# Output projection: sums of weight quadrants made by accumulating transfers from GpSimd's queue instead of by VectorE

## The chip, the cores and the metric

The kernel runs on one core of one Trainium2 chip. The metric is the time of one execution on the device in microseconds (us). A core has TensorE (PE), VectorE (DVE), ScalarE (ACT), GpSimd (POOL) and SyncE (SP), each with an instruction queue of its own that is worked off in order, and 16 DMA engines that carry the transfers which those queues issue. Engines wait for each other by semaphores.

## What is computed

A decoder layer over 512 tokens of width 2048 in float32: windowed attention and a gated DeltaNet branch, side by side, are merged and go through an output projection.

```python
y_a = a_out @ w_o_swa
y_b = o.reshape(B, T, DN_VAL).astype(x.dtype) @ w_o_dn
y = jax.nn.sigmoid(mg_a) * y_a + jax.nn.sigmoid(mg_b) * y_b
return x + gate * (y @ w_out)
```

The change touches only the last product, `y @ w_out`, with `y` of 512 x 2048 and `w_out` of 2048 x 2048.

## The kernel before

Every large product is made in three matmul passes: `split` (L52 and L53) cuts a float32 tile into a rounded high part, which ScalarE writes (`whi`), and a low part, which VectorE writes as source minus high part (`wlo`). `mm3` (L240 to L242) then multiplies high by high, high by low and low by high into the same PSUM tile.

`finish` makes the merged `y` column tile by column tile, and then calls `output`. There the last product is made by a scheme with seven quadrant products in place of eight. The four quadrants of `w_out` are halves of its rows by halves of its columns; `load` brings three of them at a time as two 1 MB tiles each: slot "a" (tile `raw`, from a pool of two buffers that the earlier stages used too), slot "b" (`rawb`) and slot "c" (`rawc`). The work runs over two halves `n` of each quadrant's columns. In each half the seven products come in the order m1, m7, m5, m2, m6, m4, m3 (the list `order`), and each product has four pieces `p` of 128 x 1024 weights. `piece(slot, p)` is such a piece. One piece feeds 12 matmuls.

The weights of m7, m6 and m4 are sums of quadrants. They are made in place, piece by piece: for m7, a becomes a + b, and b then becomes b + c; for m6, a becomes a + c; for m4, b becomes b + a. m5 uses the a that m7's first sum left. Slot b is loaded anew after m7 (for m2), and a, b and c are loaded for the second half after m4 and m3 (`after`). VectorE makes the sums, in `prep`, just before the piece is split.

`prep(i + 2)` is called after the first half of item `i`, so weights are prepared two pieces ahead of PE; `whi` and `wlo` have three buffers. Beside this run `combos` (L1309 to L1319), a generator that is advanced once an item and makes the sums of `y`'s quadrants on VectorE (tiles `ya`, `yc`, split into `hh`, `hl`), and `evict` and `columns` (L1397 to L1433), which take finished products out of PSUM on VectorE and ScalarE, scale them by the gate, add the residual `x` on GpSimd (L1400) and store the result by SP.

The instructions of each engine are placed by a scheduler from the order in which the program is written and from the dependences between tiles; semaphore waits follow from those. All transfers of the kernel before are issued by SP.

Of the kernel before, what the change touches and what calls it, by code (L numbers as in the profile page):

```python
# [11 lines left out]
ALU = mybir.AluOpType  # L12
# [24 lines left out]
class Layer:  # L37
# [1288 lines left out]
    def output(self, es, wk, A):  # L1326

        tc, nc, a = self.tc, self.nc, self.a
# [4 lines left out]
        def load(slot, c, r, nchunk):  # L1333

            for i in range(2):
                if slot == "a":
                    t = self.wraw.tile([P, 2048], F32, tag="raw", name="raw")
                else:
                    t = fr.tile([P, 2048], F32, tag=f"{slot}{i}", name=f"raw{slot}")
                nc.sync.dma_start(out=t, in_=a["w_out"][2 * c + nchunk, 2 * r + i])  # L1340
                slots[slot, i] = t

        piece = lambda slot, p: slots[slot, p // 2][:, (p % 2) * 1024 : (p % 2) * 1024 + 1024]

        def add(x, y):
            def f(p):
                nc.vector.tensor_tensor(out=piece(x, p), in0=piece(x, p), in1=piece(y, p), op=ALU.add)

            return f

        order = [
            ("m1", "a11", "a", []),
            ("m7", "s3", "b", [add("a", "b"), add("b", "c")]),
            ("m5", "s1", "a", []),
            ("m2", "a12", "b", []),
            ("m6", "s2", "a", [add("a", "c")]),
            ("m4", "a22", "b", [add("b", "a")]),
            ("m3", "s4", "c", []),
        ]
        items = [(n, m, p) for n in range(2) for m in range(7) for p in range(4)]  # L1360
# [6 lines left out]
        def prep(i):  # L1367
            if i >= len(items):
                return
            n, m, p = items[i]  # L1370
            name, _, slot, sums = order[m]
            for f in sums:
                f(p)
            hi = self.whl.tile([P, 1024], F32R, tag="whi", name="whi")
            lo = self.whl.tile([P, 1024], F32R, tag="wlo", name="wlo")
            self.split(hi, lo, piece(slot, p))
            ready[i] = (hi, lo)
            for s, c, r in after.get((name, p), []):
                if name == "m7":
                    load(s, c, r, n)  # L1380
                elif n == 0:
                    load(s, c, r, 1)
# [53 lines left out]
        for i in range(2):  # L1436
            prep(i)
        for i, (n, m, p) in enumerate(items):
            name, s, slot, _ = order[m]
            if p == 0:  # L1440
                for t in range(2):
                    m7 = name == "m7"
                    ps[name, t] = pf.tile([P, T], F32, tag=f"y{t}" if m7 else "r", name=name, bufs=1 if m7 else 6)
            hi, lo = ready.pop(i)
            ah, al = A[s]
            for kk in range(2):
                kt = 2 * p + kk
                w = slice(kk * T, kk * T + T)
                for t in range(2):
                    tsl = slice(t * P, (t + 1) * P)  # L1450
                    self.mm3(ps[name, t], (ah[:, kt, tsl], al[:, kt, tsl]), (hi[:, w], lo[:, w]), kt == 0, kt == 7)
                if kk == 0:
                    prep(i + 2)
                    for f in todo:
                        evict(*f)
                    todo = []
                    next(side, None)
            if p == 3:
                todo.append((n, name))
# [108 lines left out]
```

## Time and profile before

| | |
|---|---|
| time, median of 3 runs | 2930.38 us (2930.1 to 2932.3) |
| span of the profiled execution | 2929.7 us, mean granted PE clock 0.995 |
| median less that span | 0.7 us |
| busy: PE, VectorE, ScalarE, GpSimd | 2870.6, 1787.2, 1085.1, 243.0 us |
| moved by DMA | 451.11 MB, mean 154 GB/s |
| first and last matmul of the output projection start at | 2752.3 and 2921.4 us |

The page gives the profiled execution by its span, from the first to the last instruction; the runs are timed without a profile. Rows of a timeline give start, duration, engine, source line, operation, output and inputs, and in brackets the idle time before and what ended it. The rows of windows give, for each engine, the busy time and the number of instructions in a stretch, then PE's granted clock, the mean busy share of the 16 DMA engines and what they moved.

### The profile page before, as it was taken

Reading aid. Unit: us, or ns where it says so; the run is one execution under the profiler, and the core shown is the slowest. Engines: PE = TensorE matmul, PEld = TensorE weight load, DVE = VectorE, ACT = ScalarE, POOL = GpSimd, SP = SyncE. Lnnn points to the kernel's source line nnn. Section 1 sums busy time; section 2 is a strip of 40 time slices with the busy share of each in tenths; the row PEclk is TensorE's granted clock in tenths of the full one; section 3 lists DMA queues with packets and bytes.
Section 4 is the critical chain, followed back from the end, with each engine's and each line's share of the span. In section 5 each row is a group of like instructions: output and inputs, shape, how many; then the busy total and the mean of one; then the engine's idle time right before and its main releaser. Section 6 shows DMA issues by size and latency. Waiting matters only on the chain.

```text
span 2929.7 us, 38073 instructions
## 1 busy us (share of the span) xinstructions
PE 2870.6 (98%) x14556; PEld 2351.2 (80%) x14556; DVE 1787.2 (61%) x2915; ACT 1085.1 (37%) x2113; POOL 243.0 (8%) x204
## 2 busy tenths in 40 slices
PE   8899999999999999999999999999999999999988
PEld 6677888888888888888888788888787877888867
DVE  6775998777776545544444553434655655553697
ACT  4355333333334333333333322212343443432343
POOL 0022211100000110000000000000100000000022
PEclk9999999999999999999999999999999999999999
DMA  9747555633334533333332675554322223375562
GB/s 387 281 147 219 163 169 159 203 109 111 125 113 134 160 116 124 115 122 109 123 109 100 235 263 182 186 172 141 105 89 94 85 89 103 119 262 172 173 194 97
DMA packets 175046, 451.11 MB, mean 154 GB/s; under 512 B 72433, under 2 KB 74993, under 8 KB 138897
## 3 DMA queue, kind: packets, MB, share of 16 engines
q1 hardware_dynamic: 174866, 448.70, 46.1%
q8 instruction: 114, 1.87, 0.3%
q14 instruction: 66, 0.54, 0.1%
HBM read 386.95 MB, written 59.45 MB: 152 GB/s over the span
## 4 chain that ended last, share of the span: by engine, by line
PE 84%; DVE 3%; DMA 2%; issue 1%; ACT 1%; POOL 1%; SPq 0%; POOLq 0%; DVEq 0%; ACTq 0%
PE mm L240 24%; PE mm L242 24%; PE mm L241 24%; DVE wlo L53 1%; PE S L1208 1%; PE pv L918 1%; PE po L937 1%; PE O L1259 1%; PE pP L274 1%; PE po L936 1%; PE pd L933 1%; PE pp L908 1%; PE m L241 1%; PE m L242 1%; PE m L240 1%
## 5 line engine op out<-in xcount | busy, mean ns | idle before, releaser
L240 PE MATMUL mm<-hh,whi 128*128 128x512 f32 x2784 | 1130.7, 406 | 2.3 <-ACT whi L52 1.6
L242 PE MATMUL mm<-hh,wlo 128*128 128x512 f32 x2784 | 1089.6, 391 | 1.3 <-DVE wlo L53 1.3
L241 PE MATMUL mm<-hl,whi 128*128 128x512 f32 x2784 | 1087.3, 391 | 0.0
L53 DVE TENSOR_TENSOR wlo<-raw,whi 128x1024 fp32r<-128x1024 f32 (+1 forms) x452 | 554.4, 1229 | 491.5 <-ACT whi L52 481.7
L52 ACT CAST whi<-raw 128x1024 fp32r<-128x1024 f32 (+1 forms) x452 | 470.7, 1044 | 972.9 <-PE mm L241 927.3
L242 PEld LDWEIGHTS mm<-hh,wlo 128*128 128x128 f32 x2784 | 522.6, 188 | 115.1 <-DVE wlo L53 2.2
L240 PEld LDWEIGHTS mm<-hh,whi 128*128 128x128 f32 x2784 | 523.7, 188 | 112.3 <-issue 8.4
L241 PEld LDWEIGHTS mm<-hl,whi 128*128 128x128 f32 x2784 | 524.2, 188 | 98.7 <-issue 0.4
L240 PE MATMUL mm<-oh,whi 128*128 128x512 f32 x512 | 200.6, 393 | 2.6 <-ACT oh L52 1.7
L242 PE MATMUL mm<-oh,wlo 128*128 128x512 f32 x512 | 199.4, 390 | 0.5 <-DVE wlo L53 0.5
L241 PE MATMUL mm<-ol,whi 128*128 128x512 f32 x512 | 199.5, 390 | 0.1
L865 POOL TENSOR_TENSOR qe<-qe,yq 128x512 f32<-128x512 f32 x32 | 51.4, 1624 | 902.7 <-DMA qe<-eg_rows 836.9
L714 POOL TENSOR_TENSOR E<-E,neg_g 128x512 f32<-128x512 f32 x64 | 78.4, 1224 | 476.2 <-DMA E<-g_rows 342.8
L240 PEld LDWEIGHTS mm<-oh,whi 128*128 128x128 f32 x512 | 96.0, 188 | 24.8 <-ACT oh L52 3.0
L241 PEld LDWEIGHTS mm<-ol,whi 128*128 128x128 f32 x512 | 96.1, 188 | 22.2 <-DVE ol L53 1.3
L764 DVE TENSOR_TENSOR A<-A,atmp 128x62 f32<-128x62 f32 (+30 forms) x124 | 112.9, 911 | 1.5
L242 PEld LDWEIGHTS mm<-oh,wlo 128*128 128x128 f32 x512 | 96.1, 188 | 20.9 <-DVE wlo L53 1.3
L757 DVE TENSOR_TENSOR atmp<-A 128x62 f32<-128x62 f32 (+30 forms) x124 | 109.3, 882 | 1.5
L911 DVE SCALAR_TENSOR_TENSOR r<-pp,neg_eg,vt 128x128 f32<-128x128 f32 x96 | 29.2, 346 | 78.8 <-PE pp L908 77.6
L1232 ACT ACTIVATE sm<-sm,mx,rs 128x256 f32<-128x256 f32 (+1 forms) x128 | 71.7, 561 | 3.3 <-DVE mx L1227 3.3
L580 DVE SCALAR_TENSOR_TENSOR yv<-mm,convh,yv 128x511 f32<-128x511 f32 (+2 forms) x96 | 71.5, 745 | 1.6
L241 PE MATMUL m<-wlo,hh 128*128 128x512 f32 x128 | 51.8, 404 | 10.1 <-DVE wlo L53 10.1
(331 smaller groups left out, 3145.6 us busy)
## 6 DMA issues: line engine op xcount, KB each, us to landing
raw<-in_w_ch SPq DMA_DIRECT2D x158, 1024.0 KB
wa<-in_w_ada_ss SPq DMA_DIRECT2D x32, 1024.0 KB
raw<-in_w_od SPq DMA_DIRECT2D x32, 1024.0 KB
E<-g_rows SPq DMA_DIRECT2D x64, 256.0 KB
gw<-in_w_ada_gate SPq DMA_DIRECT2D x16, 1024.0 KB
raw<-in_w_os SPq DMA_DIRECT2D x16, 1024.0 KB
qe<-eg_rows SPq DMA_DIRECT2D x32, 256.0 KB
o_d<-zh SPq DMA_DIRECT2D x32, 256.0 KB
```

Of the source, the lines that this page charges most:

```text
L52: self.nc.scalar.copy(out=hi, in_=src)
L53: self.nc.vector.tensor_tensor(out=lo, in0=src, in1=hi.bitcast(F32), op=ALU.subtract)
L240: nc.tensor.matmul(ps, lhsT=wh, rhs=xh, start=first, stop=False)
L241: nc.tensor.matmul(ps, lhsT=wh, rhs=xl, start=False, stop=False)
L242: self.last_mm = nc.tensor.matmul(ps, lhsT=wl, rhs=xh, start=False, stop=last).ins
L274: self.nc.tensor.transpose(dst[:, c * P : (c + 1) * P], src_cols(c), self.ident)
L580: nc.vector.scalar_tensor_tensor(out=y[:, s:], in0=ps[:, : T - s], scalar=w[:, j : j + 1], in1=y[:, s:], op0=ALU.mult, op1=ALU.add)
L714: nc.gpsimd.tensor_tensor(out=E, in0=E, in1=ng, op=ALU.add)
L757: eng.tensor_tensor(out=t, in0=A[:, m : m + 1, m + 1 :].to_broadcast([P, m, n]), in1=A[:, :m, m : m + 1].to_broadcast([P, m, n]), op=ALU.mult,
L764: eng.tensor_tensor(out=A[:, :m, m + 1 :], in0=A[:, :m, m + 1 :], in1=t, op=ALU.add)
L865: nc.gpsimd.tensor_tensor(out=qf, in0=qf, in1=q, op=ALU.mult)
L1232: nc.scalar.activation(t, t, AF.Exp, scale=r[:, h : h + 1], bias=mx[:, h : h + 1], accum_out=den[:, h : h + 1])
```

## The change

The 32 VectorE additions (four sums of four pieces in each of the two halves) are taken out. In their place GpSimd issues 32 accumulating transfers from one on-chip buffer to another: `out += in`, 128 rows of 4 KB, 512 KB each. A sum is issued as soon as the piece's last use before it has been split: the two sums for m7 stand with m1's pieces, the sum for m6 with m5's and the sum for m4 with m2's, that is, four items earlier for m7 and eight for m6 and m4. In `prep` the sums now come after the split and ahead of the reloads.

```diff
-        def add(x, y):
-            def f(p):
-                nc.vector.tensor_tensor(out=piece(x, p), in0=piece(x, p), in1=piece(y, p), op=ALU.add)
-
-            return f
-
         order = [
-            ("m1", "a11", "a", []),
-            ("m7", "s3", "b", [add("a", "b"), add("b", "c")]),
-            ("m5", "s1", "a", []),
-            ("m2", "a12", "b", []),
-            ("m6", "s2", "a", [add("a", "c")]),
-            ("m4", "a22", "b", [add("b", "a")]),
+            ("m1", "a11", "a", [("a", "b"), ("b", "c")]),
+            ("m7", "s3", "b", []),
+            ("m5", "s1", "a", [("a", "c")]),
+            ("m2", "a12", "b", [("b", "a")]),
+            ("m6", "s2", "a", []),
+            ("m4", "a22", "b", []),
             ("m3", "s4", "c", []),
         ]
...
             name, _, slot, sums = order[m]
-            for f in sums:
-                f(p)
             hi = self.whl.tile([P, 1024], F32R, tag="whi", name="whi")
             lo = self.whl.tile([P, 1024], F32R, tag="wlo", name="wlo")
             self.split(hi, lo, piece(slot, p))
             ready[i] = (hi, lo)
+            for x, y in sums:
+                nc.gpsimd.dma_start(out=piece(x, p), in_=piece(y, p), accum_op=ALU.add)
             for s, c, r in after.get((name, p), []):
```

## The prediction

> **What bounds the kernel now.** I read the page first, for which engine holds the span.
>
> ```profile
> PE 2870.6 (98%) x14556; PEld 2351.2 (80%) x14556; DVE 1787.2 (61%) x2915; ACT 1085.1 (37%) x2113; POOL 243.0 (8%) x204
> ...
> q1 hardware_dynamic: 174866, 448.70, 46.1%
> ...
> PE 84%; DVE 3%; DMA 2%; issue 1%; ACT 1%; POOL 1%; SPq 0%; POOLq 0%; DVEq 0%; ACTq 0%
> ```
>
> PE (TensorE) is busy for 98% of the span and makes 84% of the chain that ended last, so only what PE loses in the changed stage can be won. The page has one queue for all data, that of SP's transfers: GpSimd (POOL) issues none before the change. Next, the stage itself: when PE starts each product, and how long it would take undisturbed.
>
> ```profile
> 2752.27 0.39 PE L240 MATMUL m<-whi,a11h 128*128 128x512 f32 x1
> ...
> 2763.15 0.39 PE L240 MATMUL m<-whi,s3h 128*128 128x512 f32 x1
> ...
> 2843.27 0.39 PE L240 MATMUL m<-whi,a11h 128*128 128x512 f32 x1
> ...
> 2854.15 0.39 PE L240 MATMUL m<-whi,s3h 128*128 128x512 f32 x1
> ...
> 2867.26 0.39 PE L240 MATMUL m<-whi,hh 128*128 128x512 f32 x1
> ```
>
> Each half of the output columns runs m1, m7, m5, m2, m6, m4, m3. In the first half m1 starts at 2752.27 and m7 at 2763.15: 48 matmuls in 10.88 us, 0.227 us each, 2.72 us for each of a product's four pieces. From there to m1 of the second half is 80.12 us, where six products need 6 x 10.88 = 65.3: **14.8 us are lost**. In the second half m7 takes 13.11 us (2.2 lost). The rest is the last row of this view, and loses nothing (5 x 10.88 = 54.4):
>
> ```profile
> core 0: us, PE busy (x) PEld busy (x) DVE busy (x) ACT busy (x) POOL busy (x), PEclk, DMA share, GB/s
> 2744.00:2769.00 25.00, 25.00 (x112) 20.64 (x111) 23.90 (x36) 11.76 (x19) 0.00 (x0) 1.00 0.52 160
> 2763.15:2843.27 80.12, 69.99 (x290) 55.44 (x289) 75.47 (x115) 36.53 (x56) 7.73 (x5) 0.94 0.65 210
> 2774.00:2812.00 38.00, 34.56 (x148) 26.79 (x146) 35.41 (x65) 20.50 (x35) 0.00 (x0) 1.00 0.52 149
> 2841.00:2860.00 19.00, 18.86 (x83) 15.28 (x82) 18.92 (x20) 6.52 (x8) 11.60 (x2) 1.00 0.42 125
> ...
> 2867.26:2921.80 54.54, 54.54 (x241) 44.87 (x239) 44.48 (x45) 20.07 (x20) 11.65 (x6) 1.00 0.31 103
> 2824.00:2836.00 12.00, 12.00 (x54) 9.95 (x53) 10.92 (x14) 4.23 (x5) 1.60 (x2) 1.00 0.93 356
> 2866.00:2875.00 9.00, 9.00 (x42) 7.44 (x41) 7.63 (x7) 2.85 (x3) 0.00 (x0) 1.00 0.90 297
> ```
>
> In the window where PE loses, VectorE (DVE) is busy for 75.47 of 80.12 us. The waits name it too:
>
> ```profile
> PE m L241 <- DVE wlo L53: 11.6, 6, 5.9
> ```
>
> All of PE's waiting in the stage is for the low part of a split weight piece. The longest wait costs more than itself:
>
> ```profile
> 2816.94 0.80 PE L241 MATMUL m<-wlo,hh 128*128 128x512 f32 x1 [5.95 <-DVE wlo L53]
> ...
> 2823.08 0.40 PE L241 MATMUL m<-wlo,hh 128*128 128x512 f32 x1
> ...
> 2840.64 0.50 PE L241 MATMUL m<-wlo,hh 128*128 128x512 f32 x1 [1.74 <-DVE wlo L53]
> ```
>
> From 2816.94 to 2823.08 PE starts 15 matmuls, 14 intervals in 6.14 us where 3.2 are normal: 3.0 us of low clock after the 5.95 us wait. After the 1.74 us wait there is none. So the change can win 14.8 + 2.2 = 17.1 us at the most: 2913.3.
>
> **Part 1, what goes: 32 additions on VectorE.**
>
> ```profile
> L1347 DVE TENSOR_TENSOR raw<-raw,rawb x8: 1214/1218/1225, 2744.4 to 2855.0; 128x1024 f32<-128x1024 f32 x8
> ...
> L1347 DVE TENSOR_TENSOR rawb<-rawb,raw x8: 1208/1224/2297, 2807.8 to 2883.8; 128x1024 f32<-128x1024 f32 x8
> ```
>
> These are the first and the last of four such rows of 8. 16 stand in each half, 16 x 1.22 = 19.5 us. In the first half that is more than the 14.8 us that PE loses, so every loss there whose cause is VectorE's queue can go. The 1.74 us before 2840.64 I keep, since it stands among the evictions of m6 and m4, which stay on VectorE.
>
> **Part 2, what comes: 32 accumulating transfers of 512 KB on GpSimd's queue.** No row shows one. What a transfer costs here is bounded by SP's.
>
> ```profile
> 2803.97 2.82 DMA ya<-y_d
> ```
>
> That is a 256 KB load, from issue to landing, where little else ran. The windows 2824 to 2836 and 2866 to 2875 give the rate of full engines: 356 / 0.93 = 383 and 297 / 0.90 = 330 GB/s, mean 356. So 256 KB are 0.74 us of moving and about 2.1 us are fixed. 512 KB (524,288 bytes) are 1.47 us of moving for each time that they pass. A sum has two sources, so two reads for one write. The low bound is one pass: 1.47 us of the engines' time, 3.6 us to landing. The high bound is four passes, 5.9 us. I take **two passes: 2.95 us of the engines and 5.05 us to landing**, as reading both operands is the least that is added to a copy; this is an estimate. The issue on GpSimd I put inside the fixed part.
>
> The Trainium skill (DMA: Bandwidth & Descriptors, Anatomy of one DMA) fits a plain GpSimd-issued transfer by 2.0 us plus its bytes over 436 GB/s, which for 512 KB is an estimate of 3.2 us. By that figure the change would end as the first rival below; no run here shows such a transfer yet.
>
> **Part 3, where they stand.** The sums are issued one product early: those for m7 right after m1's pieces are split, those for m6 after m5's, those for m4 after m2's. The last two groups (eight transfers) have two products' time. The first group is eight transfers with one product's time, and b += c must wait until a += b has read b. GpSimd's queue is in order, so each b += c also holds what stands behind it. By the changed program's order, GpSimd's queue in the second half is
>
> ```
> a+=b p0, out add (m1), a+=b p1, b+=c p0, a+=b p2, b+=c p1,
> out add (m5), b+=c p2, out add (m5), a+=b p3, b+=c p3
> ```
>
> "out add" is the residual addition L1400 of the first half's last results, which waits for its own load.
>
> **First half, m7.** The window is from the first split of m1 to when m7's last piece must be summed.
>
> ```profile
> 2742.92 1.22 DVE L53 TENSOR_TENSOR wlo<-raw,whi 128x1024 fp32r<-128x1024 f32 x1
> 2838.71 1.04 ACT L52 CAST whi<-raw 128x1024 fp32r<-128x1024 f32 x1 [1.67 <-DVE m L1429]
> ```
>
> The first split ends at 2744.1. PE reads the last piece at 2763.15 + 3 x 2.72 = 2771.3, and the split takes 1.04 + 1.22 + 0.1 = 2.4 us: 2768.9. In these 25 us other transfers hold the engines for 0.52 x 25 = 13.0 us; eight sums need 8 x 2.95 = 23.6. 36.6 us of work in 25 is **11.6 us late**. I expect it as two long waits, each with 3.0 us of low clock: 17.6 us.
>
> **First half, the rest.** From m5's first split to m4's last piece are about 3 x 10.88 + 3 x 2.72 less 2.1 of landing, 38.7 us. Other transfers hold 0.52 x 38 = 19.8 us, the eight sums 23.6: 43.4, or 4.7 late, with 3.0 of clock. Of the 14.8 us lost before, 1.74 stays, and these 7.7 come: 5.4 us are won. First half: 17.6 - 5.4 = +12.2 us.
>
> **Second half, m7.** On GpSimd:
>
> ```profile
> 2828.82 1.29 POOL L1400 TENSOR_TENSOR c<-c,x 128x512 f32<-128x512 f32 x1 [9.06 <-DVE c L1397]
> ...
> 2843.88 1.99 POOL L1400 TENSOR_TENSOR m<-m,x 128x512 f32<-128x512 f32 x1 [4.38 <-DMA x<-in_x]
> 2850.39 12.59 POOL L1400 TENSOR_TENSOR m<-m,x 128x512 f32<-128x512 f32 x2 [4.52 <-DMA x<-in_x]
> ```
>
> I replay the queue with before's times, one sum on the engines at a time. The cast at 2838.71 lets m1's first split end at 2841. a+=b p0 lands at 2846.1. a+=b p1 goes after the 1.99 us addition, moves to 2848.9, lands at 2851.0; b+=c p0 lands at 2853.9, and with its split is 2.2 us late for 2854.15. a+=b p2 lands at 2856.9; b+=c p1 at 2859.8. b+=c p2 waits for a+=b p2 and holds the second out add, which ends at 2858.9 (2 us, VectorE being freer). Only then go a+=b p3, landing at 2865.7, and b+=c p3, landing at 2870.8: its split ends at 2873.2, PE wants it at 2854.15 + 8.16 = 2862.3: **10.9 us late**. Other transfers hold 0.42 x 19 = 8.0 us in that window; half of it I add (4.0), since the chain leaves the engines idle in part. With two waits' low clock (6.0), less the 2.2 us lost there before: +18.7. Later in this half the engines are at 0.31 and PE loses nothing before; I add nothing. It is covered by two products' time, and without this cover the 4.7 us of the first half is its price.
>
> **Sum:** 12.2 + 18.7 = 30.9 us. The profiled span is 2929.7 us, 0.7 under the median of the runs, 2930.4; the sum goes on the median: **2961 us**.
>
> **The rivals.** (1) *One pass: sums as cheap as copies.* Then eight are 11.8 us and fit the 12.0 us left free in the first half's window, and in the second half a+=b p3 goes at 2854.4, b+=c p3 lands at 2861.6, is split at 2864.0, 1.7 us late where 2.2 were lost. 14.8 - 1.74 + 0.5 = 13.6 us won: 2917. Against it: the in-order queue with three waits in it, and the two reads. (2) *Three or four passes.* At 4.4 us the first half's m7 is 35.2 + 13.0 - 25 = 23.2 late, m4 16.3; in the second half 35.2 + 8.0 in the 16.8 us to the last landing is 26.4 late, m4 about 5.5; five low clocks 15; less 15.3 of the losses that go: +71, 3001. Four passes: about 3050. (3) *GpSimd starves at issuing.* Two additions took it 12.59 us at 2850.39 beside a busy VectorE, against 1.29 for one at 2828.82. If issuing slows alike to 6.3 us, eight issues and two additions need 63 us in a window of 19: 44 late, and in the first half 50 in 25: 25 late; with clocks and gains about 2990. The Trainium skill (SBUF — State Buffer, Who interferes with whom) says that a VectorE operation with two SBUF inputs holds up GpSimd's reads, which the 12.59 us agree with, but that GpSimd's writing of descriptors is shut out only by VectorE's two-port modes, which its tensor_tensor doesn't have. By that the price falls away and the sum stays; so this rival gets little. (4) *No change:* a price near 1.7 us of engine time, where m7's new waits equal the stalls that go: 2930. That the sums stay on VectorE is excluded: the changed program has 32 transfers on GpSimd's queue and no L1347.
>
> **How the numbers follow.** The forecast (two passes, 2945 to 2980) 0.50; three or more passes 0.20; starved issue 0.10; one pass 0.12; no change 0.08. About 0.2%, 5.9 us, is what a measurement of this kernel can tell from none. Faster 0.12, same 0.08, slower 0.80. All slow cases but the worst half of (2) lie under 3010, and a low end of 2926 takes in (4) and leaves out (1).
>
> **What would show it.** Right: VectorE's busy time in the stage falls by some 39 us; PE waits in m7 of both halves for splits that wait for GpSimd's transfers, over 4 us at a time, with low clock behind; the 5.95 us wait before m4 shrinks; GpSimd's queue carries 16.8 MB or more. Wrong: sums landing within 4 us of their issue, m7 in 10.9 us, the second half unchanged; or m7 on time and m4 late, which would put the price on the shared engines rather than on the chain.

## The result and the profile after

The changed kernel takes **2967.47 us** (median of 4 runs, 2966.51 to 2969.87) against 2931.34 us for the kernel before on the same chip (4 runs, 2930.1 to 2932.97): the ratio is **1.0122, 95% interval 1.011 to 1.0134**, slower by 36 us. The profiled execution took 2966.51 us, its span is 2963.5 us, 33.8 us longer than before's. The page of the kernel after, busy times, queues (packets, MB, share of 16 engines) and the chain that ended last:

```profile
PE 2883.0 (97%) x14556; PEld 2356.0 (80%) x14556; DVE 1748.7 (59%) x2883; ACT 1084.8 (37%) x2113; POOL 256.3 (9%) x236
...
q1 hardware_dynamic: 174866, 448.70, 45.4%
q0 software_dynamic: 4608, 16.78, 3.0%
...
PE 84%; DVE 5%; DMA 5%; issue 2%; ACT 2%; POOL 1%; SPq 0%; POOLq 0%; DVEq 0%; ACTq 0%
```

VectorE is relieved as planned: 1787.2 - 1748.7 = 38.5 us. A second queue, GpSimd's, carries 16.78 MB in 32 transfers; 3.0% of 2963.5 us is 88.9 us, so **one sum holds the 16 engines for 2.78 us**. On the chain that ended last, transfers have grown from 2% to 5%. The waits of the stage (2740 to 2964) say where they stand in it; the columns are us in total, times, and the longest:

```profile
ACT whi L52 <- DMA rawb<-rawc: 31.1, 5, 13.3
POOL rawb L1371 <- DMA raw<-rawb: 30.9, 7, 7.0
...
PE m L241 <- DVE wlo L53: 16.9, 16, 3.4
PE m L240 <- ACT whi L52: 16.5, 4, 7.3
DVE ya L1313 <- DMA ya<-y_d: 16.1, 9, 3.6
```

Read from above: the first chained sum (a += b) holds the second on GpSimd's queue, the second (b += c) holds the cast of a piece on ScalarE, and that cast holds PE. Before, PE waited 11.6 us in this stage, all for `wlo`; now it is 33.4 us, half of it for `whi`. The last line is another path, which the prediction did not have: loads of `y` that come late to VectorE. The windows of the stage, with the columns in the first line:

```profile
core 0: us, PE busy (x) PEld busy (x) DVE busy (x) ACT busy (x) POOL busy (x), PEclk, DMA share, GB/s
2744.00:2769.00 25.00, 21.78 (x92) 17.02 (x91) 10.67 (x18) 7.80 (x12) 5.78 (x7) 0.98 0.94 215
2764.00:2788.00 24.00, 16.90 (x51) 11.55 (x50) 12.81 (x22) 9.05 (x15) 3.29 (x4) 0.80 0.92 253
...
2858.00:2877.00 19.00, 11.68 (x51) 9.12 (x49) 7.58 (x9) 3.15 (x3) 7.11 (x7) 0.91 1.01 256
2877.00:2901.00 24.00, 16.04 (x48) 11.16 (x48) 6.68 (x6) 6.01 (x7) 5.60 (x6) 0.78 0.81 218
```

Around both m7 the DMA engines stand at 0.81 to 1.01 of their time (the view's sum can come out a little over 1), where before they stood at 0.52 and 0.42, and VectorE, which had been busy for 23.90 of 25 us, is busy for 10.67. PE's granted clock falls to 0.80 and 0.78. PE's own rows at the five longest waits:

```profile
2781.70 0.79 PE L240 MATMUL m<-whi,s3h 128*128 128x512 f32 x1 [2.29 <-ACT whi L52]
...
2809.28 0.79 PE L241 MATMUL m<-wlo,a12h 128*128 128x512 f32 x1 [2.59 <-DVE wlo L53]
...
2848.42 0.50 PE L241 MATMUL m<-wlo,hh 128*128 128x512 f32 x1 [3.42 <-DVE wlo L53]
...
2876.53 0.80 PE L240 MATMUL m<-whi,s3h 128*128 128x512 f32 x1 [7.32 <-ACT whi L52]
...
2895.19 0.80 PE L240 MATMUL m<-whi,s3h 128*128 128x512 f32 x1 [5.83 <-ACT whi L52]
```

Three of the five are in m7 (`s3h`), one is in m2 (`a12h`) and one in the first half's last products. The long waits of the second half can be followed on GpSimd's queue,

```profile
2858.49 0.88 POOL L1371 DMA_DIRECT2D raw<-rawb  x1 [1.98 <-DVE wlo L53]
...
2867.72 0.86 POOL L1371 DMA_DIRECT2D rawb<-rawc  x1 [3.51 <-DMA raw<-rawb]
...
2879.85 1.18 POOL L1371 DMA_DIRECT2D raw<-rawb  x1
2888.05 0.86 POOL L1371 DMA_DIRECT2D rawb<-rawc  x1 [7.01 <-DMA raw<-rawb]
```

and on ScalarE's:

```profile
2875.43 1.04 ACT L52 CAST whi<-rawb 128x1024 fp32r<-128x1024 f32 x1 [13.29 <-DMA rawb<-rawc]
...
2894.09 1.04 ACT L52 CAST whi<-rawb 128x1024 fp32r<-128x1024 f32 x1 [8.34 <-DMA rawb<-rawc]
```

For piece 0, a += b goes out at 2858.49, b += c only at 2867.72, and the cast at 2875.43 ends the 7.32 us wait of PE: 9.2 and 7.7 us for two sums in a chain. The same for the last piece, 2879.85 to 2888.05 to 2894.09, ends the 5.83 us wait. What the engines carried meanwhile is told by the view of the DMA between 2858 and 2877:

```profile
q0 software_dynamic: 603, 2.22, 58.8%
q1 hardware_dynamic: 1035, 2.64, 42.5%
```

58.8% of 19 us is 11.2 us, four sums of 2.78 us; SP's transfers take 42.5%, 8.1 us. Together they fill the window, and a sum that would land in 4.6 us when it is alone lands later:

```profile
DMA to landing us min/median/max: 4.6/7.2/9.4
```

To compare kernels I use one table: how long PE took for each product, from the start of its first matmul to that of the next product's, so that a wait before m7's first piece counts to m1. Undisturbed a product takes 10.9 us and the three products m6, m4, m3 32.6. In the second half, m5, m2 and the last three took 10.9, 10.9 and 32.6 us in every kernel, and are left out: the last eight transfers there cost nothing.

| kernel | m1 | m7 | m5 | m2 | m6 to m3 | m1, 2nd half | m7, 2nd half | stage | kernel, us |
|---|---|---|---|---|---|---|---|---|---|
| before | 10.9 | 10.9 | 13.6 | 10.9 | 44.7 | 10.9 | 13.1 | 169.4 | 2931.3 |
| after | 12.6 | 23.7 | 11.2 | 17.0 | 42.1 | 18.4 | 24.7 | 204.1 | 2967.5 |
| E1: m7's sums on VectorE | 10.9 | 10.9 | 12.1 | 18.2 | 41.0 | 16.9 | 14.1 | 178.5 | 2942.1 |
| E2: only m7's by transfer | 10.9 | 23.2 | 12.9 | 10.9 | 42.4 | 19.0 | 23.8 | 197.4 | 2963.3 |
| E3: plain copies | 10.9 | 13.4 | 10.9 | 15.9 | 42.5 | 16.9 | 19.6 | 184.5 | 2948.8 |
| E4: no sums | 10.9 | 10.9 | 12.6 | 12.2 | 43.9 | 11.0 | 10.9 | 166.8 | 2932.8 |
| E5: a + b without the chain | 12.1 | 16.1 | 13.7 | 17.6 | 42.9 | 10.9 | 26.4 | 194.1 | 2955.7 |
| E6: residual additions on VectorE | 12.8 | 20.9 | 12.2 | 17.3 | 37.0 | 22.3 | 20.6 | 197.7 | 2958.9 |
| E8: before, third buffer | 10.9 | 11.4 | 10.9 | 10.9 | 40.9 | 10.9 | 15.1 | 165.3 | 2928.2 |
| E9: no sums, third buffer | 10.9 | 10.9 | 11.0 | 12.3 | 32.7 | 10.9 | 10.9 | 153.9 | 2916.8 |
| E10: GpSimd adds in the first half | 10.9 | 11.3 | 17.3 | 18.6 | 36.7 | 11.0 | 14.8 | 175.1 | 2936.7 |
| E11: E1, third buffer | 10.9 | 11.6 | 14.8 | 15.0 | 37.1 | 10.9 | 12.9 | 167.6 | 2930.4 |
| E12: after, third buffer | 14.1 | 24.6 | 15.2 | 16.2 | 33.2 | 16.2 | 23.7 | 197.7 | 2960.4 |
| E13: E8, m4's sums of the first half by transfer | 10.9 | 11.4 | 10.9 | 13.3 | 40.7 | 11.6 | 12.9 | 166.1 | 2927.4 |

The stage begins up to 4 us earlier or later from one profile to the next, for reasons before it, so stages are compared by their length. The change makes it longer by 204.1 - 169.4 = 34.7 us, of which the span shows 33.8. Each stage is that of one profiled execution, and the runs of one kernel differ by 3 to 13 us, so a difference of a few us between two stages is not clear of noise. Where an experiment was timed, the kernel before took 2931.2 to 2934.4 us in the median.

### The profile page after: what moved, and what is told of

The parts are those of the page before. It is cut to its first block, busy times and chain, and to the rows that moved or that the text cites. A ratio compares the mean times of both kernels' runs of the same rounds, so it can differ in the third digit from the quotient of the medians.

```text
span 2963.5 us, 38139 instructions
## 1 busy us (share of the span) xinstructions
PE 2883.0 (97%) x14556; PEld 2356.0 (80%) x14556; DVE 1748.7 (59%) x2883; ACT 1084.8 (37%) x2113; POOL 256.3 (9%) x236
## 3 DMA queue, kind: packets, MB, share of 16 engines
q0 software_dynamic: 4608, 16.78, 3.0%
## 4 chain that ended last, share of the span: by engine, by line
PE 84%; DVE 5%; DMA 5%; issue 2%; ACT 2%; POOL 1%; SPq 0%; POOLq 0%; DVEq 0%; ACTq 0%
PE mm L240 24%; PE mm L242 24%; PE mm L241 24%; DVE wa L414 1%; DVE wlo L53 1%; DMA raw<-rawb 1%; PE S L1208 1%; PE pv L918 1%; PE po L937 1%; PE O L1259 1%; PE pP L274 1%; ACT whi L52 1%; DMA oraw<-o_d 1%; PE pd L933 1%; PE pp L908 1%
## 5 line engine op out<-in xcount | busy, mean ns | idle before, releaser
L240 PEld LDWEIGHTS mm<-oh,whi 128*128 128x128 f32 x512 | 96.1, 188 | 23.7 <-ACT oh L52 1.8
```

Of the source, the lines that this page charges most:

```text
L240: nc.tensor.matmul(ps, lhsT=wh, rhs=xh, start=first, stop=False)
```

## The experiments

Account A is the prediction's: a sum costs two passes on the shared engines, and what is chained comes late. The other letters are rivals, as each expectation tells. Kernels for which no interval is given were run once.

**E1 and E2: which of the transfers cost the time.** E1 gives m7's sums back to VectorE, E2 gives back the others.

```diff
-            ("m1", "a11", "a", [("a", "b"), ("b", "c")]),
+            ("m1", "a11", "a", []),
...
+            if name == "m7":
+                for x, y in (("a", "b"), ("b", "c")):
+                    nc.vector.tensor_tensor(out=piece(x, p), in0=piece(x, p), in1=piece(y, p), op=ALU.add)
```

> The two sums for m7 are back on VectorE, just ahead of m7's splits as before; the sums for m6 and m4 stay on GpSimd's queue. Theory A (the loss is in m7, whose eight sums have one product's time for some 22 us of engine work): m1 and m7 of both halves run as before the change, the 32.8 us that they lost go, and the kernel takes 2925 to 2937 us. Rival B (the added traffic costs wherever it falls): about half of the loss stays, 2945 to 2955 us, with waits in m2, m6 and m4.

Measured: 2942.12 us (2938.8 to 2943.4), ratio to before 1.0034 [1.002, 1.0048].

```diff
-            ("m5", "s1", "a", [("a", "c")]),
-            ("m2", "a12", "b", [("b", "a")]),
+            ("m5", "s1", "a", []),
+            ("m2", "a12", "b", []),
...
+            for x, y in {"m6": [("a", "c")], "m4": [("b", "a")]}.get(name, []):
+                nc.vector.tensor_tensor(out=piece(x, p), in0=piece(x, p), in1=piece(y, p), op=ALU.add)
```

> The mirror image: only the sums for m7 are transfers, those for m6 and m4 are VectorE additions as before. Theory A: m7 loses what it lost in the changed kernel, m2 is no longer late (6 us), the wait before m4 is back (some 6 us with the low clock): 2962 to 2970 us. Rival B: half of the loss goes with half of the transfers, 2945 to 2955 us.

Measured: 2963.28 us. Against before's stage, m7's transfers add 28.0 us (E2) and the others 9.1 (E1); together that is 37.1, near the 34.7 of the whole change. So about three quarters of the loss are m7's. But the others, which the prediction let win time, lose it: in E1 m2 takes 18.2 us, though none of its own weights is summed. PE's and VectorE's rows in E1 show how. VectorE:

```profile
2789.79 0.43 DVE L1313 TENSOR_TENSOR ya<-ya,yc 128x256 f32<-128x256 f32 x1 [2.18 <-DMA ya<-y_d]
...
2790.80 1.22 DVE L53 TENSOR_TENSOR wlo<-rawb,whi 128x1024 fp32r<-128x1024 f32 x1
```

PE:

```profile
2792.07 0.80 PE L241 MATMUL m<-wlo,a12h 128*128 128x512 f32 x1 [4.22 <-DVE wlo L53]
```

the load of `y`, from the view of the chain between 2775 and 2800:

```profile
2782.69 7.08 DMA ya<-y_d
```

and the queues between 2780 and 2800:

```profile
q0 software_dynamic: 698, 2.53, 65.6%
q1 hardware_dynamic: 1152, 2.10, 32.9%
```

PE waits 4.22 us for a split of m2. That split stands on VectorE's in-order queue behind an addition for the *next* products (`ya`), and that addition waits for a load of `y`. The load took 7.08 us to landing, where the one that the prediction shows took 2.82; the sums meanwhile hold 65.6% of engines that are full. A transfer that has two products' time for itself still costs, by what it makes late for others.

**E3: the price of the sum.** The transfers stay, without the accumulation.

```diff
-                nc.gpsimd.dma_start(out=piece(x, p), in_=piece(y, p), accum_op=ALU.add)
+                nc.gpsimd.dma_start(out=piece(x, p), in_=piece(y, p))
```

> The changed kernel with the same 32 transfers in the same places as plain copies (out = in); so the sums are left out. Theory A (a sum passes the engines about twice): the engines' time for one falls from 2.78 to about 1.5 us, eight take 12 us, and m7 is nearly on time: 2917 to 2935 us. Rival C (the price is the in-order queue with its waits for landings and the fixed part of each, not the bytes): time to landing stays at 6 us and over, 2955 to 2965 us.

Measured: 2948.82 us. E3's page has for GpSimd's queue

```profile
q0 software_dynamic: 4608, 16.78, 1.5%
```

that is 1.5% of 2946.3 us over 32 transfers, 1.38 us for a copy of 512 KB where a sum takes 2.78: twice, for the same bytes counted. That a sum costs the engines two copies is shown. The median landings of E3's four groups are 5.3, 3.8, 4.6 and 3.0 us, after's 8.3, 6.0, 7.2 and 5.1. And still E3 is 17 us slower than before: had a sum cost no more than a copy, the change would have lost.

**E4: what VectorE's relief is worth.** The transfers go, VectorE's additions do not come back.

```diff
-            for x, y in sums:
-                nc.gpsimd.dma_start(out=piece(x, p), in_=piece(y, p), accum_op=ALU.add)
```

> All sums are left out, by transfer and by addition: what VectorE's relief alone is worth. Forecast's bound: 14.8 us of the first half less the 1.74 us before m3, and 2.2 us of the second half go: about 2916 us. Rival D (the first half's losses come from the loads of y's quadrants and the evictions, not from the additions): 2924 us or more.

Measured: 2932.76 us, a stage of 166.8 against 169.4. To take 39 us of work off VectorE shortens the stage by 2.6 us, and the one time measured shows no gain. From m7 to m3 of the first half VectorE's busy time falls from 75.47 to 63.23 us, and PE needs 79.6 us in place of 80.1. E4's waits of the stage:

```profile
PE m L241 <- DVE wlo L53: 10.1, 6, 3.5
```

PE waits for VectorE's splits nearly as long as before (11.6). And VectorE's own waits, from the same view:

```profile
DVE ya L1313 <- DMA ya<-y_d: 9.4, 8, 3.5
...
DVE u L1413 <- DMA out<-c: 4.1, 1, 4.1
...
DVE c L1416 <- DMA out<-c: 3.0, 1, 3.0
```

It is not at work but standing: for loads of `y`, and for stores of results (`out<-c`) that must free a buffer before the next result may be written. Those buffers (`ya`, `c`, `u` and others) are one group of two, tag "m".

**E5: without the landing of a + b in the chain.** m7's first sum takes b from HBM, so that b += c no longer waits for it.

```diff
+                src = a["w_out"][2 + n, p // 2][:, (p % 2) * 1024 : (p % 2) * 1024 + 1024] if (x, y) == ("a", "b") else piece(y, p)
-                nc.gpsimd.dma_start(out=piece(x, p), in_=piece(y, p), accum_op=ALU.add)
+                nc.gpsimd.dma_start(out=piece(x, p), in_=src, accum_op=ALU.add)
```

> The changed kernel with the addend of a += b read from w_out in HBM instead of from slot b. Then b += c has no landing of a += b to wait for and GpSimd's queue is not held, while bytes and order stay. The output's first half of m1 and m7 (43.1 us in the second half after the change, 24.0 before) tells: theory A' (in the second half the loss is the in-order chain of landings; with copies of half the engine time 12.5 of its 19 us stayed): m1 and m7 of the second half fall to about 32 us, and the kernel to 2950 to 2958 us. Theory A (the engines' time alone): nothing falls, 2962 to 2970 us.

Measured: 2955.67 us. m1 and m7 of the first half fall from 36.3 to 28.2 us, of the second from 43.1 to 37.3. Some of the lateness is the chain, but most of the second half's loss (37.3 against 21.8 undisturbed) remains without it. E3, which keeps the chain and halves the engine time, comes to 24.3 and 36.5. In the second half neither alone accounts for the loss. Without the chain the sums stand on the engines together (shares of 0.85 between 2845 and 2865, 1.06 from there to 2885), and b += c takes 11.2 us to landing in the median, against 6.0 after.

**E6: GpSimd's queue without its additions.** The prediction let an addition of the first half's results hold the last a += b in the queue.

```diff
-            nc.gpsimd.tensor_tensor(out=src, in0=src, in1=x, op=ALU.add)
+            nc.vector.tensor_tensor(out=src, in0=src, in1=x, op=ALU.add)
```

> The changed kernel with the residual additions of the results (L1394) on VectorE, so that GpSimd's queue holds transfers only. Forecast's replay has the last a += b of the second half wait for two such additions: by it m1 and m7 of the second half fall by some 5 us, 2960 to 2963 us. Rival: the additions only fill time in which the queue waits for landings anyway, 2966 to 2970 us.

Measured: 2958.88 us. m1 and m7 of the second half still take 42.9 us (43.1 after). That step of the replay was no cause. The kernel is faster by another part, m6 to m3, 42.1 to 37.0; why was not tried.

**E8 and E9: the two buffers.** Tag "m" gets a third buffer, in the kernel before (E8) and in E4 (E9).

```diff
-                p = wk.tile([P, T], F32, tag="m", name="ya")
+                p = wk.tile([P, T], F32, tag="m", bufs=3, name="ya")
```

and alike at the four other tiles of that tag.

> The kernel before, with three instead of two buffers for the tiles m, ya, c11, u2 and c22; sums as before on VectorE. Theory E (PE's loss in the first half comes from VectorE's in-order queue standing at tiles whose loads or stores have not landed, not from the number of its operations): the 14.8 us lost from m7 to m3 of the first half shrink by 5 to 10 us, 2921 to 2927 us. Rival F (VectorE's work itself): within 2 us of before.

Measured: 2928.19 us (2926.0 to 2930.7), ratio 0.9991 [0.9982, 1.0001].

> As the kernel without any sums (sums left out), with the third buffer of the run beside it. Theory E: the buffers and the sums together were what PE lost, nearly all of the 17 us goes, 2914 to 2920 us. Rival: the loads of y's quadrants stay late whatever the buffers, 2926 to 2932 us.

Measured: 2916.82 us; what PE still waits in E9's stage is

```profile
PE m L241 <- DVE wlo L53: 0.8, 1, 0.8
```

The buffer alone shortens the stage by 4.1 us, the sums alone by 2.6, both by 15.5: 153.9 us, where undisturbed 14 products take 152.3. The times say the same: 2932.8 without the sums, 2928.2 with the buffer, 2916.8 with both, against 2931 to 2932 before. The loss before had **two causes that cover each other**, the sums on VectorE and the waits for buffers.

**E10: additions on GpSimd.** E8, with the first half's sums for m6 and m4 made early by GpSimd itself.

```diff
-            for f in sums:
-                f(p)
+            if n or name == "m7":
+                for f in sums:
+                    f(p)
...
+            early = {"m5": [("a", "c")], "m2": [("b", "a")]}.get(name, []) if n == 0 else []
+            for x, y in early:
+                nc.gpsimd.tensor_tensor(out=piece(x, p), in0=piece(x, p), in1=piece(y, p), op=ALU.add)
```

> The kernel before with the third buffer, and the first half's sums for m6 and m4 as GpSimd additions issued one or two products early (beside m5's and m2's pieces), where the change had transfers; the other sums stay on VectorE. If VectorE's relief is worth something once the buffers are there (theory E, from 2928 with the buffer to 2917 without any sums): m7 to m3 of the first half lose 4 us at most, 2918 to 2924 us. Rival: GpSimd and VectorE hold each other up (12.59 us for two additions before), no gain over 2928 us or a loss.

Measured: 2936.73 us, ratio 1.0021 [1.0012, 1.0031]; m5 takes 17.3 and m2 18.6 us. E10's rows of GpSimd and of VectorE at one of the eight:

```profile
2782.19 2.51 POOL L1381 TENSOR_TENSOR raw<-raw,rawc 128x1024 f32<-128x1024 f32 x1 [2.17 <-DVE wlo L53]
```

```profile
2782.36 2.62 DVE L1313 TENSOR_TENSOR ya<-ya,yc 128x256 f32<-128x256 f32 x1
```

VectorE's instruction is a small one, 0.42 us in the other kernels. It begins behind GpSimd's addition and ends 0.28 us after it: VectorE stood while GpSimd added. The same is seen at all eight, with some 2.6 us each. So GpSimd's additions take VectorE's time, and 2.51 us of it in place of 1.22.

**E11 and E12: the parts again, with the third buffer.** E11 is E1 and E12 the kernel after, each with that buffer.

> m7's sums on VectorE, the sums for m6 and m4 as accumulating transfers, and the third buffer. Theory G (transfers for m6 and m4 delay the reload of slot b for m2 and the loads of the second half, on full DMA engines): m2 of the first half takes over 14 us, m1 of the second half over 14, and the kernel 2930 to 2940 us. Rival: with the buffer these 16 transfers are covered and VectorE's relief shows, 2918 to 2926 us.

Measured: 2930.40 us, a stage of 167.6. m5 and m2 lose 3.9 and 4.1 us still (14.8 and 15.0), so that loss is not the buffers'; the 6.0 us that E1 lost in m1 of the second half are gone (10.9).

> The changed kernel with the third buffer. Theory A (m7's eight sums against one product's time, on full engines): m1 and m7 still take over 33 us in the first half and over 40 in the second, 2955 to 2963 us. Rival (the loss was the buffers' after all): 2935 to 2945 us.

Measured: 2960.42 us. m1 and m7 take 38.7 and 39.9 us (36.3 and 43.1 after): what m7 loses is the transfers', with or without the buffer. m6 to m3 falls to 33.2, 0.6 over undisturbed, which the relief of VectorE was to bring; but E11, with the same relief there, comes to 37.1, and the difference was not followed.

**E13: the transfers that should hide.** E8, and by transfer only b += a of the first half, issued behind m6's splits, where no reload of slot b stands beside it.

```diff
-            for f in sums:
+            for f in sums if n or name != "m4" else []:
...
+            if n == 0 and name == "m6":
+                nc.gpsimd.dma_start(out=piece("b", p), in_=piece("a", p), accum_op=ALU.add)
```

> The kernel before with the third buffer (as in the earlier experiment, stage 165.3 us), and only the four sums b += a for m4 of the first half by transfer, issued behind the splits of m6, one product early; every other sum on VectorE. Theory A (what the first half's last transfers cost lies where they meet the reload of slot b and where eight stand together; four alone, 4 x 2.78 = 11.1 us of the engines over 10.9 us with no reload beside them, are hidden): m2 stays at 10.9 us, m6 to m3 falls from 40.9 us by up to 4 x 1.22 = 4.9 us, stage 160 to 164, kernel 2922 to 2927. Rival H (a transfer's 6 to 8 us to landing cannot be hidden behind one product anywhere; m4 comes late as m7 did): m6 to m3 over 43 us with waits of PE before m4, stage 167 or more, kernel 2930 or more.

Measured: 2927.36 us (2923.84 to 2932.95) against 2934.35, ratio 0.9981 [0.9971, 0.9991]. PE's waits between 2801 and 2843 in E13:

```profile
PE m L241 <- DVE wlo L53: 2.5, 2, 1.7
PE m L240 <- ACT whi L52: 2.2, 4, 1.3
```

H is wrong: nothing long stands before m4. Three of the four sums are hidden behind one product, and the last, which went out late (2819.91) behind a residual addition on GpSimd, costs PE 1.2 us. A is not shown either: m6 to m3 stays (40.7 against 40.9), m2 takes 13.3, and the stage is no shorter than E8's (166.1 against 165.3); but the profiled execution took 2930.92 us, 3.6 over this kernel's median. At 0.19% under the kernel before it is the fastest here that computes the whole, but its interval overlaps E8's, so what the four transfers add to the buffer is not settled.

## Why the prediction was right, and where not

The forecast was 2961 us, slower by 31; it is 2967.5, slower by 36. The steps:

- **What bounds the kernel: half right.** What PE lost was all there was to win: E9, with hardly a wait of PE left, comes to 2916.8, and the ceiling was put at 2913.3. Wrong is the step that reads the cause from VectorE's 75.47 busy us of 80.12 ("every loss there whose cause is VectorE's queue can go"). E4 takes the work away and wins 2.6 of 17.1 us. Before, the queue stood for only 4.7 of the 80.12 us; with the additions gone it stood for 16.4 of 79.6, mostly for loads of `y` and for stores that free a buffer. One limit hid the other, and the share of busy time does not show the second.
- **The price of a sum: right on the engines, too small to landing.** 2.95 us were estimated for two passes, 2.78 measured, and E3's 1.38 for one. To landing 5.05 were put, and 7.2 is the median, 4.6 the least: the estimate holds for a sum that has the engines to itself. The Trainium skill (DMA: Bandwidth & Descriptors, Anatomy of one DMA) gave an estimate of 3.2 us for a plain transfer; E3's least disturbed group, at 3.0, agrees, and its others are later.
- **First half, m7: mechanism right, size a little high.** +17.6 were forecast; m1 and m7 rose from 21.8 to 36.3, +14.5. The engines were full, as the sum of 36.6 us of work in 25 had it (shares 0.94 and 0.92). The form was another: not two long waits but eight, none over 2.3 us and 8.2 together, where 11.6 were put. Most of the other 6 us is low clock, as forecast, but here it followed waits much shorter than the 5.95 us that the prediction read: after 2.11 us before 2766.66 the granted clock was 0.50 between 2768 and 2771, after 2.29 us before 2781.70 it was 0.54 between 2781 and 2788.
- **First half, the rest: the step that failed.** -5.4 us were forecast (7.7 for late sums, 13.1 won by relief). m5 to m3 went from 69.2 to 70.3, **+1.1**. The relief of 13.1 was worth little without the third buffer (E4, E12), and the sums' price did not fall on m4 but on m2, by loads of `y` that stood ahead of a split in VectorE's queue (E1). The step saw the eight sums only in the place where they are used.
- **Second half, m7: size right, way partly wrong.** +18.7 were forecast, +19.1 measured (24.0 to 43.1), and that the two are so close is partly luck. The replay had piece 0 late by 2.2 us and piece 3 by 10.9; PE waited 7.32 for piece 0 and 5.83 for piece 3. Piece 0 set off later, since m1's own split came late (its a += b went out 0.4 us after PE began m1, at 2858.5; the replay had it 2 us ahead), and its two sums took 16.9 us from the first issue to the cast, not 12.9. Of SP's 8.0 us only half was added, as the chain would leave gaps; it left none (58.8% and 42.5%). And the addition that was to hold the last a += b was no cause (E6).
- **The later transfers of the second half at nothing: right.** m5 to m3 take 54.4 us before and after. Between 2909 and 2922 the sums alone hold the engines at 0.99, each lands in 4.7 to 5.0 us, and PE is busy for 13.00 of 13 us: full engines cost nothing where nothing waits for them.

The sum was 30.9 us, the stage shows 34.7: 3.1 too much in the first half's m7, 6.5 too little in its rest, 0.4 too little in the second. Part of the agreement is errors that cancel.

The rivals: one pass was priced at 2917, and E3, which is one pass, takes 2948.8; it would not have been faster. Three or four passes and no change are excluded by the 2.78 us. Starved issue is excluded by the rows of GpSimd: an issue takes 0.85 to 1.21 us beside VectorE's splits and its additions for `y`, which is what the Trainium skill (SBUF — State Buffer, Who interferes with whom) had said against that rival.

What stays open: how the second half's 21.3 us divide into chain and full engines, and why E6 won time in m6 to m3.

## What to carry to other kernels

Before work is taken off an engine that looks full, ask what its in-order queue would stand for without that work: which loads, which buffers. Here two causes covered each other, the waits of the kernel before showed little of the second, and only their removal together showed a gain. Work that goes to the DMA engines is priced in their time, at two copies for a sum, and added to what they carry in *that* stretch. Where loads that something waited for stood beside the sums on full engines (E1), the loads came late, and the price appeared wherever they headed an in-order queue. Two transfers in a chain cost two full landings, under load 6 to 9 us each, so they need far more than one product's time.

## What the runs showed that was not expected

An accumulating transfer between on-chip buffers holds the engines twice as long as a copy (2.78 and 1.38 us for 512 KB), as the prediction had estimated, while the byte count of its queue is the same 16.78 MB and does not show it. And GpSimd and VectorE hold each other up in both directions: in the kernel before two GpSimd additions took 12.59 us beside VectorE, in E10 an instruction of VectorE that needs 0.42 us took 2.62, until GpSimd's addition had ended. The second agrees with the Trainium skill (SBUF — State Buffer, SBUF: two separate sides), by which, of a VectorE operation with two SBUF inputs and a GpSimd operation that reads SBUF, the one that starts first holds the shared ports for its whole instruction.
